# Gate projections of two branches by seven block products, in a two-layer trunk on one core

## The chip, the cores and the metric

The kernel is one program on one core of a Trainium2 chip. Its engines run their own instruction streams in order and meet at semaphores: PE (TensorE, the matmuls; its weight loads are shown as PEld), DVE (VectorE), ACT (ScalarE), POOL (GpSimd) and SP (SyncE, which issues all DMAs here). The metric is device time in microseconds (us): the median of three runs of the kernel before is 2673.18 us (2672.58 to 2675.56).

## The reference, cut to what matters

Two layers, each with 1024 tokens and width 1024. Three branches (g = 0, 1, 2) give `y_g` of width 512 each; a sigmoid gate per branch and output column weighs their projections.

```
h = rms_norm(x, norm_w);  p = h @ w_in                      # [1024, 1024] @ [1024, 9180]
... y_a, y_b, y_c from p: sparse attention (g 0), stick-breaking attention (g 1), mLSTM (g 2)
proj  = einsum('bsgc,gcd->bsgd', branches, w_branch)
gates = sigmoid(merge.reshape(b, s, 3, 1024))               # merge: the last 3 * 1024 columns of p
mixed = sum(gates * proj, axis=2)
x     = x + mixed @ w_out
```

So the gates are three products of 1024 x 1024 by 1024 x 1024 per layer that need nothing but `h`.

## The kernel before, in words

**Arithmetic.** A float32 matrix is cut into a high part of type fp32r and a low part (the rest). A product is three passes, high by high, high by low and low by high (`PASSES`), all summed in one bank of PSUM. With blocks of 128 on the contraction, a tile of 128 columns by 512 tokens takes 24 matmuls of 128x512 (8 blocks, 3 passes), or 12 over half of the contraction. Cutting a tile costs a copy on ACT (the high part; the profile shows it as CAST) and two subtractions of 128x256 on POOL (`pool_tt`; the low part).

**Stages of a layer.** Small projections and index scores (p1); mLSTM and, beside it, a search for thresholds on DVE and ACT (p2); stick-breaking attention (p3); sparse attention (p4); then the branch projections, times the gates, and the output product, which is done in seven block products already (p5). `h`, transposed and cut, stays in SBUF as `hT`: in each of two parts eight blocks of 128 by two halves of 512 tokens (`mov(b, k, th)`).

**The work ahead.** The gates depend on `h` alone, so the 24 matmuls of each gate tile are done while attention runs, as work that PE takes when nothing more urgent is ready. There are 48 such tiles a layer (3 branches, 8 column blocks `d`, 2 token halves `th`), 1152 matmuls. They have two PSUM banks of their own (`psf`) and ten SBUF tiles (`fill`). The gate goes through a sigmoid on ACT and into DRAM (`gate_d`), and is read back in p5.

**The order.** The body is not issued as it runs. It is recorded as a list (`Log`), and a planner (`Plan.run`) then plays the list through with costs for each operation, gives out buffers, and fixes one order per engine. Among what is ready an engine takes the lowest key. For work ahead on PE the key is its place in the list plus `AHEAD_SHIFT`, so it comes behind nearly all else; on the other engines the key is its bare place. `Plan.emit` issues all of it from one line, so nearly every row of the profile names L533; the shape and the type tell the operations apart. In names, `t` is a tile of its own, `s` a large tile that two halves share, `d` a tile in DRAM.

Of the kernel before, what the change touches and what calls it, by code (L numbers as in the profile page):

```python
# [23 lines left out]
DEPTH = 2  # L24
N_HALF = 21
N_SLAB = 35
N_FILL = 10
N_PSF = 2
TK_ACT = (3, 4, 5)
EPS = 1e-6  # L30
# [3 lines left out]
PASSES = ((0, 0), (0, 1), (1, 0))  # L34
# [3 lines left out]
C_MLQ, C_MLK, C_MLV, C_IF, C_MLO, C_MLZ, C_MERGE = 3540, 4052, 4564, 5076, 5084, 5596, 6108  # L38
# [49 lines left out]
MARGIN = {"half": 2, "slab": 2}  # L88
STEP = 100
SPARE = {"ps": 2}  # L90
AHEAD = (2, 1, 0)
AHEAD_SHIFT = 7700
LOOK = {"half": 400, "slab": 400, "ps": 300}
EXTRA = 0.0
# [117 lines left out]
class Plan:  # L212
# [3 lines left out]
    def __init__(self, log, info, caps):  # L216
        self.info, self.caps = info, caps
        prio = log.prio
        ops = []
        n = len(log)  # L220
        self.deps = [set() for _ in range(n)]
        acc, users = {}, {}
        for k, (eng, meth, args, kw) in enumerate(log):
            o = Op()
            o.eng, o.meth, o.args, o.kw = eng, meth, args, kw
            ins, outs = operands(meth, args, kw)
            o.cost = cost(eng, meth, args, kw, ins, outs)
            o.table = table_of(args) if eng == "ACT" else None
            o.port = holds_port(eng, meth, args, kw, ins, outs)
            o.bytes = nbytes(outs[0]) if eng == "SP" else 0  # L230
            o.tiles = []
            ops.append(o)
            for wr, lst in ((False, ins), (True, outs)):
                for a in lst:
                    nm = a.tensor.name
                    if nm not in info:
                        continue
                    if nm not in o.tiles:
                        o.tiles.append(nm)
# [12 lines left out]
        for r, k in enumerate(by):  # L252
            at[k] = r
        self.ops = [ops[k] for k in by]
        self.deps = [{at[k2] for k2 in self.deps[k]} for k in by]
        self.users = {nm: sorted(at[k] for k in u) for nm, u in users.items()}
        self.early = {at[k] for k in log.early}
        self.prio = [prio[k] for k in by]
        self.place = by
        self.n = n  # L260
        for k, d in enumerate(self.deps):
            if d and max(d) > k:
                raise ValueError("the priorities do not follow the data")

    def run(self):
        n, ops, info, caps = self.n, self.ops, self.info, self.caps
# [3 lines left out]
            for k2 in d:  # L270
                succ[k2].append(k)
        pri, early = self.prio, self.early
        key = [pri[k] if k not in early or ops[k].eng == "PE" else self.place[k] for k in range(n)]
        first = {nm: u[0] for nm, u in self.users.items()}
        last = {nm: u[-1] for nm, u in self.users.items()}
        left = {nm: len(u) for nm, u in self.users.items()}
# [2 lines left out]
        for nm in left:  # L279
            c = info[nm][1]  # L280
# [20 lines left out]
        f = 0  # L301
# [312 lines left out]
def body(log, tiles, caps, x_in, w_in, w_uk, w_uv, kvn, conv_w, ib, fb, mln, w_br, w_out, nrm, fnrm,  # L614
         rope_t, out, stop=None, dbg=None):
    V, S, G, PE, SY = (Engine(log, e) for e in ("DVE", "ACT", "POOL", "PE", "SP"))
# [9 lines left out]
    def half(dt=F32, n=520):  # L626
        return tiles.new("half", [128, n], dt)
# [5 lines left out]
    def fill(dt=F32):  # L633
        return tiles.new("fill", [128, 512], dt)
# [151 lines left out]
    for tb in range(8):  # L786
        x = slab()
# [13 lines left out]
    for l in range(DEPTH):  # L801
        wl = w_in[l]

        def cols(c, n, _w=wl):
            return _w[:, c:c + n]

        def mov(b, k, th, _h=hT):
            return _h[b][k][th][:, :512]
# [51 lines left out]
        for i in range(4):  # L860
# [8 lines left out]
            d = ikd[i // 2][:, (i % 2) * 256:(i % 2) * 256 + 256].rearrange("p (t e c) -> p t e c", t=2, e=2)  # L869
# [13 lines left out]
        for tb in range(2, 8):  # L883
            v = iq[tb // 2][:, (tb % 2) * 256:(tb % 2) * 256 + 256].rearrange("p (h c) -> p h c", h=4)
            q = half(F32R)
# [3 lines left out]
            p = pst("tr")  # L889
# [29 lines left out]
        for th in range(2):  # L919
            ss = small([128, 8], name="ssk", bufs=2)  # L920
            for j in range(2):
                w = pb[2 * th + j][:, :424].rearrange("p (t c) -> p t c", t=2)[:, :, 0:128]
                q = half()
# [5 lines left out]
            p = pst("tr")  # L929
# [6 lines left out]
            q = half()  # L936
# [101 lines left out]
            SY.dma_start(f(y_d[g][0][blk][:, t0:t0 + n]), f(hi[:, :n]))  # L1038
            SY.dma_start(f(y_d[g][1][blk][:, t0:t0 + n]), f(lo[:, :n]))

        gate_d = {}
        log.ahead, log.shift = True, AHEAD_SHIFT
        for g in AHEAD:
            for d in range(8):
                W = [[], []]
                for hb in range(2):
                    st, wh, wl_ = fill(), fill(F32R), fill(F32R)
                    SY.dma_start(st[:, :512].rearrange("p (k c) -> p k c", k=4),
                                 cols(C_MERGE + g * 1024 + d * 128, 128)[hb * 512:hb * 512 + 512, :]
                                 .rearrange("(k p) c -> p k c", p=128))  # L1050
                    S.copy(wh[:, :512], st[:, :512])
                    pool_tt(wl_, st, f(wh), ALU.subtract, 512)
                    W[0].append(wh)
                    W[1].append(wl_)
                for th in range(2):
                    p = pst("psf")
                    i = 0
                    for a, b in PASSES:
                        for k in range(8):
                            PE.matmul(p, W[a][k // 4][:, (k % 4) * 128:(k % 4) * 128 + 128], mov(b, k, th),  # L1060
                                      start=(i == 0), stop=(i == 23))
                            i += 1
                    t = fill()
                    S.activation(t[:, :512], p, AF.Sigmoid)
                    gate_d[g, d, th] = dram([128, 512])
                    SY.dma_start(gate_d[g, d, th], t[:, :512])
        log.ahead, log.shift = False, 0

        if stop == "p1":
# [25 lines left out]
        p = pst("tr")  # L1095
# [5 lines left out]
        p = pst("tr")  # L1101
# [8 lines left out]
        p = pst("tr")  # L1110
# [21 lines left out]
        p = pst("tr")  # L1132
# [7 lines left out]
        for h in range(4):  # L1140
            W1 = load_w([(cols(C_MLQ + h * 128, 128), 0), (cols(C_MLK + h * 128, 128), 128)])
            cv = {}
            for j in range(2):
                raw = [half(), half()]
                for th in range(2):
                    p = pst("mm")
# [6 lines left out]
                for th in range(2):  # L1153
                    a = half()
                    blk = 4 * j + h
# [10 lines left out]
            if h % 2 == 0:  # L1166
                W2 = load_w([(cols(C_MLV + h * 128, 256), 0)])
                vq = []
                for q in range(4):
                    p = pst("mm")  # L1170
# [418 lines left out]
            return g, p  # L1589

        def wm(g, ct):
            return (None if g in AHEAD else load_w([(cols(C_MERGE + g * 1024 + ct * 256, 256), 0)]),
                    load_w([(w_br[l, g][:, ct * 256:ct * 256 + 256], 0)], nk=4))

        last = l == DEPTH - 1
# [142 lines left out]
```

## Time and profile before

| | |
|---|---|
| median of 3 runs | 2673.18 us |
| profiled execution | 2675.59 us, its span 2673.8 us |
| PE busy | 2641.5 us, 99% |
| DVE, ACT, POOL busy | 1749.8, 1466.0, 1100.4 us (65, 55, 41%) |
| DMA | 243.16 MB on SP's queue, 29.5% of 16 engines |
| granted TensorE clock, mean over the span | 0.999 of full speed |

Busy time of PE runs from the start of a matmul to its modelled end, and the next one starts before that end, so a row's mean for one matmul is longer than the step from one matmul to the next. The step is read from a stretch in which PE does one kind of work without a break. A wait that is shorter than the overlap of two matmuls shows as busy PE.

### The profile page before, as it was taken

The numbers are of one execution on the slowest core, as the hardware profiler recorded it, in microseconds if no ns is written. First come the engines' busy times: TensorE is split into PE (matmuls) and PEld (weight loads), VectorE is DVE, ScalarE is ACT, GpSimd is POOL, SyncE is SP. The second block draws the span as 40 slices with busy tenths as digits, with TensorE's granted clock in tenths as the row PEclk, the third lists the DMA queues.
The fourth block names the chain that finished last, engine by engine and source line by source line (L and its number), as shares of the span: only waits on it lengthen the run. The fifth ranks groups of instructions, "written<-read, shape, count | busy, mean of one in ns | idle before, by whom it ended". The sixth has DMA issues, their size and how long they took to land.

```text
span 2673.8 us, 41885 instructions
## 1 busy us (share of the span) xinstructions
PE 2641.5 (99%) x14676; PEld 2233.9 (84%) x14676; DVE 1749.8 (65%) x4059; ACT 1466.0 (55%) x2971; POOL 1100.4 (41%) x1445
## 2 busy tenths in 40 slices
PE   8999999999999999999999999999999999999998
PEld 7888888888888888888898888888888878888886
DVE  5829789667596753426866397996666776723278
ACT  4737873545476866512445469634556577764123
POOL 4343344332342534444814253432342444433536
PEclk9999999999999999999999999999999999999999
DMA  4322232212132315564204132231111322256531
GB/s 126 90 51 68 76 79 68 64 52 69 35 94 64 89 55 185 192 222 150 69 25 121 32 103 52 68 93 51 55 57 34 98 76 79 65 173 234 176 118 71
DMA packets 252550, 245.83 MB, mean 92 GB/s; under 512 B 23514, under 2 KB 198580, under 8 KB 252340
## 3 DMA queue, kind: packets, MB, share of 16 engines
q1 hardware_dynamic: 252340, 243.16, 29.5%
q8 instruction: 116, 1.90, 0.3%
q14 instruction: 94, 0.77, 0.1%
HBM read 180.84 MB, written 62.26 MB: 91 GB/s over the span
## 4 chain that ended last, share of the span: by engine, by line
PE 90%; DVE 4%; ACT 3%; issue 2%; POOL 0%; DMA 0%; POOLq 0%; ACTq 0%; DVEq 0%
PE t L533 90%; DVE t L533 4%; ACT t L533 3%; POOL t L533 0%; ACT L533 0%; DMA t<-in_w_in_dram 0%; ACT s L533 0%; DMA t<-in_x_dram 0%; DVE s L533 0%; POOLq L1734 0%; ACTq L533 0%; DVEq L533 0%; POOLq L533 0%
## 5 line engine op out<-in xcount | busy, mean ns | idle before, releaser
L533 PE MATMUL t<-t,t 128*128 128x512 f32 (+5 forms) x13802 | 2497.4, 342 | 22.4 <-DVE t L533 10.0
L533 PEld LDWEIGHTS t<-t,t 128*128 128x128 f32 (+2 forms) x13674 | 2080.1, 183 | 384.2 <-DVE t L533 23.3
L533 POOL TENSOR_TENSOR t<-t,t 128x256 fp32r<-128x256 f32 (+5 forms) x956 | 767.9, 833 | 1006.5 <-ACT t L533 409.0
L533 DVE TENSOR_TENSOR t<-t,t 128x512 f32<-128x512 f32 (+12 forms) x1454 | 725.9, 528 | 586.1 <-ACT t L533 470.7
L533 ACT CAST t<-t 128x512 fp32r<-128x512 f32 (+6 forms) x991 | 504.0, 549 | 456.8 <-PE t L533 222.3
L533 ACT ACTIVATE t<-t 128x512 f32<-128x512 f32 (+5 forms) x697 | 343.3, 579 | 266.6 <-PE t L533 210.9
L533 ACT ACTIVATE t<-t,t 128x1024 bf16<-128x1024 f32 (+10 forms) x352 | 307.9, 887 | 61.0 <-DVE t L533 34.2
L533 ACT COPY t<-t 64x256 f32<-64x256 f32 (+4 forms) x300 | 113.0, 379 | 250.9 <-PE t L533 248.6
L533 DVE TENSOR_TENSOR_SCAN t<-t 128x256 f32<-128x256 f32 (+10 forms) x144 | 205.0, 1436 | 8.8 <-ACT t L533 8.6
L533 POOL TENSOR_SCALAR t<-t 64x512 fp32r<-64x512 f32 x128 | 83.2, 650 | 247.2 <-ACT t L533 169.4
L533 DVE SCALAR_TENSOR_TENSOR t<-t,t,t 128x512 f32<-128x512 f32 (+8 forms) x217 | 160.0, 766 | 18.0 <-ACT t L533 11.2
L533 PE MATMUL t<-s,t 128*128 128x512 f32 (+1 forms) x474 | 149.1, 385 | 0.0
L533 DVE TENSOR_SCALAR_CACHE_REDUCE t<-t,t 128x512 bf16<-128x512 f32 (+5 forms) x198 | 145.8, 763 | 1.1
L533 ACT ACT_TABLE_LOAD x105 | 134.7, 1283 | 14.0 <-PE t L533 6.6
L533 POOL TENSOR_SCALAR t<-t,t 128x128 f32<-128x128 f32 (+7 forms) x128 | 94.8, 749 | 110.4 <-DVE t L533 107.3
L533 DVE TENSOR_TENSOR s<-s,t 128x512 f32<-128x512 f32 (+1 forms) x98 | 69.3, 709 | 106.7 <-PE t L533 97.8
L533 DVE CUSTOM_DVE_ANT_0 t<-t,t 128x512 f32<-128x512 f32 (+3 forms) x160 | 92.1, 591 | 18.0 <-PE t L533 9.4
L533 PEld LDWEIGHTS t<-s,t 128*128 128x128 f32 x474 | 87.4, 188 | 19.0
L533 POOL TENSOR_TENSOR t<-s,s 128x256 fp32r<-128x256 f32 x50 | 52.5, 1075 | 44.8 <-issue 30.6
L533 DVE TENSOR_SCALAR t<-t,t 128x512 f32<-128x512 f32 (+12 forms) x94 | 52.8, 573 | 19.2 <-ACT t L533 11.0
L533 DVE TENSOR_SCALAR t<-t 128x1 f32<-128x1 f32 (+5 forms) x324 | 58.8, 190 | 5.9 <-ACT t L533 3.7
L533 DVE TENSOR_TENSOR t<-t 128x1 f32<-128x1 f32 (+6 forms) x224 | 59.0, 272 | 3.7 <-POOL t L533 1.0
(53 smaller groups left out, 811.5 us busy)
## 6 DMA issues: line engine op xcount, KB each, us to landing
t<-in_w_in_dram SPq DMA_DIRECT2D x192, 256.0 KB, 3.7
d<-t SPq DMA_DIRECT2D x134, 256.0 KB, 2.0
t<-d SPq DMA_DIRECT2D x133, 256.0 KB, 5.2
s<-d SPq DMA_DIRECT2D x103, 256.0 KB, 5.3
t<-in_w_in_dram SPq DMA_DIRECT2D x44, 512.0 KB, 5.2
d<-t SPq DMA_DIRECT2D x130, 128.0 KB, 1.8
t<-in_w_branch_dram SPq DMA_DIRECT2D x24, 512.0 KB, 6.0
t<-in_x_dram SPq DMA_DIRECT2D x16, 512.0 KB, 5.6
```

The costliest lines, as they stand in the source:

```text
L533: fn(*args, **kw)
```

## The change

Branch 2 (`PLAIN`) keeps its 24 matmuls a tile. For branches 1 and 0 (`AHEAD`) column blocks `d` and `d + 4` are taken as a pair, so that the product is one of 2 x 2 blocks: two halves of the columns, two of the contraction, two of the tokens. It is done in seven products of 12 matmuls in place of eight.

- Four sums of blocks of `h` (S0 to S3 here, each of four 128x512 blocks, cut into high and low) are made at the start of a layer, at four places 1200 list entries apart (`SUM_SHIFT`), and kept in DRAM (`s_d`): 64 subtractions and additions of 128x256 on POOL, 16 copies on ACT, 24 operations of 128x512 on DVE and 32 stores a layer.
- For each of the eight pairs (2 branches, 4 `d`) the sums of weights are made by POOL, cut, and partly kept in DRAM (`t1_d`, `t2_d`). Products that belong to several outputs (`p_d`, `u_d`, `v_d`) go to DRAM and come back: copied into the PSUM bank by ACT ahead of the matmuls (`S.copy(X, t)`), or added by DVE behind them (`back`).
- The products run in four phases over all eight pairs, each with one sum in the same eight `half` tiles (`ts`), which are loaded again for each phase (`sums_of`).
- Work ahead on ACT, DVE, POOL and SP gets a key that is spread over the stretch from 700 to 7800 entries behind the block (`Plan.spread`) in place of its bare place. `N_FILL` rises from 10 to 12.

```diff
-N_FILL = 10
+N_FILL = 12
...
-AHEAD = (2, 1, 0)
+PLAIN = (2,)
+AHEAD = ((1, 0),)
+SUM_SHIFT = 1200
+LATER = 0
+SPREAD = (700, 7800)
...
+    def spread(self, c):
+        a, z = next((a, z) for a, z in self.blocks if a <= c < z)
+        return z + SPREAD[0] + (c - a) / (z - a) * (SPREAD[1] - SPREAD[0])
...
-        key = [pri[k] if k not in early or ops[k].eng == "PE" else self.place[k] for k in range(n)]
+        key = [pri[k] if k not in early or ops[k].eng == "PE" else self.spread(self.place[k]) for k in range(n)]
...
+        for k in range(4):
+            log.shift = SUM_SHIFT * (k + 1)
...
+            t = both(a21, a22, ALU.add)
+            keep(1, k, t)
...
-                W = [[], []]
-                for hb in range(2):
-                    st, wh, wl_ = fill(), fill(F32R), fill(F32R)
...
+                W = [cut_w(raw(g, d, hb)) for hb in range(2)]
...
+        for gs in AHEAD:
+            pairs = [(g, d) for g in gs for d in range(4)]
+            for g, d in pairs:
+                W1 = cut_w(raw(g, d, 0))
+                Z = pst("psf")
+                gprod(Z, W1, blk(0, 0))
+                t = fill()
+                S.copy(t, Z)
+                put(p_d, (g, d), t)
+                W2 = cut_w(raw(g, d, 1))
+                gprod(Z, W2, blk(0, 4), False)
+                close((g, d, 0), Z, fill())
+            ts = [(half(F32R)[:, :512], half(F32R)[:, :512]) for _ in range(4)]
+            Sm = sums_of(0, ts)
+            for g, d in pairs:
+                r11, r12, r22 = raw(g, d, 0), raw(g, d + 4, 0), raw(g, d + 4, 1)
+                add(r12, r12, r11, ALU.subtract)
+                put(t1_d, (g, d), r12)
+                add(r12, r22, r12, ALU.subtract)
+                put(t2_d, (g, d), r12)
+                W6 = cut_w(r12)
+                X = pst("psf")
+                t = fill()
+                SY.dma_start(t, p_d[g, d])
+                S.copy(X, t)
+                gprod(X, W6, Sm, False)
+                S.copy(t, X)
+                put(u_d, (g, d), t)
+            Sm = sums_of(1, ts)
+            for g, d in pairs:
+                W5 = cut_w(bring(t1_d[g, d]))
+                X = pst("psf")
+                gprod(X, W5, Sm)
+                put(v_d, (g, d), back(X, u_d[g, d]))
+            Sm = sums_of(2, ts)
...
+            Sm = sums_of(3, ts)
...
+                S.copy(X, t)
+                gprod(X, W3, Sm, False)
+                close((g, d + 4, 0), X, t)
```

Where the order moves, first on PE, before: a piece of stick-breaking attention in the first layer with work ahead between. Each row is output <- moving operand, weights; `t410` is a `psf` bank, `t43` to `t57` are the high parts of `hT`, `t406` and `t409` low parts of weights, `t1862` holds attention logits.

```order
L533 MATMUL t410_7981<-t57_253,t408_7993 128x512
L533 MATMUL t410_7981<-t43_217,t406_7937 128x512 [waits Pool_49]
L533 MATMUL t410_7981<-t47_228,t406_7937 128x512 [waits Pool_49]
L533 MATMUL t410_7981<-t51_240,t409_8037 128x512 [waits Pool_49]
L533 MATMUL t1862_8075<-t1747_7607,t1751_7670 128x128 [waits DVE_49]
L533 MATMUL t1862_8075<-t1747_7607,t1752_7675 128x128
L533 LDWEIGHTS t2_96
L533 MATMUL t1862_8075<-t3_98,t2_96 128x128
```

The moving operand of the work ahead is always `hT`, which is there from the start of the layer, and what it waits for is cut weights.

On PE now, at the first change from S0 to S1 in the same part of the program. `s536`, `s538` and `t540` are three of the eight tiles of the sum, `t621` is the last bank of phase S0, `t627` and `t633` are the first two of phase S1, `t2099` to `t2139` are attention.

```order
L544 MATMUL t621_8623<-s536_1542,t620_8747 128x512 [waits Pool_49]
L544 MATMUL t621_8623<-s538_2263,t620_8747 128x512
L544 MATMUL t2129_8825<-t2011_8188,t2015_8273 128x256 [waits DVE_49]
L544 MATMUL t2099_8799<-t1_92,t2094_8664 128x128 [waits DVE_49]
L544 MATMUL t2098_8852<-t2100_8839,t1943_7800 128x256 [waits Activation_49]
L544 MATMUL t627_8858<-s536_1542,t625_8671 128x512 [waits DMAHW4_49]
L544 MATMUL t627_8858<-s538_2263,t625_8671 128x512 [waits DMAHW5_49]
L544 MATMUL t627_8858<-t540_3962,t625_8671 128x512 [waits DMAHW6_49]
L544 MATMUL t633_8867<-s536_1542,t631_8781 128x512
L544 MATMUL t2139_8882<-t2011_8188,t2015_8273 128x384 [waits PE_49,Activation_49]
```

Rows that repeat are left out; between the last read of the old `s536` and the first of the new one PE has 18 matmuls in all: three of 128x512, two of 128x256, one small one, eleven of 128x128 and one more of 128x256. The first row of the new phase waits for a DMA.

On SP now, the loads of S1 at that place. The first two columns of a row's operands are target and source; `d` is DRAM, and `t646` and the stores belong to other work.

```order
L544 DMA s536_1542<-d284_1476 128x512 [waits DMAHW6_49,PE_49]
L544 DMA s538_2263<-d285_2176 128x512 [waits DMAHW7_49,PE_49]
L544 DMA d262_8103<-t2067_8712 128x256 [waits DMAHW0_49,Pool_49]
L544 DMA t541_3983<-d286_3852 128x512 [waits DMAHW1_49,PE_49]
L544 DMA t543_6079<-d287_6003 128x512 [waits DMAHW2_49,PE_49]
L544 DMA t646_8784<-d583_8471 128x512 [waits DMAHW3_49,Pool_49]
L544 DMA s536_1542<-d280_1454 128x512 [waits DMAHW4_49,PE_49]
L544 DMA s538_2263<-d281_2146 128x512 [waits DMAHW5_49,PE_49]
L544 DMA t540_3962<-d282_3819 128x512 [waits DMAHW6_49,PE_49]
L544 DMA d623_8823<-t622_8514 128x512 [waits DMAHW7_49,Activation_49]
L544 DMA t542_6072<-d283_5970 128x512 [waits DMAHW0_49,PE_49]
```

Each of the eight loads waits for the last matmul that reads the old tile, and stands in one queue with stores that wait for ACT and POOL. Such a change from one sum to the next comes three times a layer; the sums themselves and their loads are new.

## Rows read from the trace of the kernel before

**Rows 1.** The page's first part: busy us, share, instructions of each engine.

```profile
PE 2641.5 (99%) x14676; PEld 2233.9 (84%) x14676; DVE 1749.8 (65%) x4059; ACT 1466.0 (55%) x2971; POOL 1100.4 (41%) x1445
```

**Rows 2.** The chain that ended last, by engine.

```profile
PE 90%; DVE 4%; ACT 3%; issue 2%; POOL 0%; DMA 0%; POOLq 0%; ACTq 0%; DVEq 0%
```

**Rows 3.** Windows: the output product of layer one; busy us (x instructions), clock, DMA.

```profile
core 0: us, PE busy (x) PEld busy (x) DVE busy (x) ACT busy (x) POOL busy (x), PEclk, DMA share, GB/s
1203.00:1270.00 67.00, 67.00 (x290) 54.19 (x289) 43.10 (x61) 13.99 (x22) 28.00 (x36) 1.00 0.45 150
```

**Rows 4.** Lines by form, PE's costliest: busy us, mean ns, idle before, releasers.

```profile
L533 PE MATMUL t<-t,t 128*128 128x512 f32 x6968 | 1823.0, 402 | 4.3 <-ACT t L533 2.7 <-DVE t L533 1.0 <-POOL t L533 0.3
```

**Rows 5.** Timeline of PE, runs of narrow matmuls: start, us, row, count.

```profile
19.81 2.63 PE L533 MATMUL t<-t,t 128*128 128x256 f32 x21
...
342.47 1.28 PE L533 MATMUL t<-t,t 128*128 128x128 f32 x10
```

**Rows 6.** Waits, of weight loads: us in total, times, longest.

```profile
PEld t L533 <- DVE t L533: 23.3, 58, 3.4
PEld t L533 <- ACT t L533: 22.5, 66, 1.9
...
PEld t L533 <- POOL t L533: 13.2, 35, 1.9
```

**Rows 7.** DMA issues by kind: count, KB each, median us to landing.

```profile
t<-in_w_in_dram SPq DMA_DIRECT2D x192, 256.0 KB, 3.7
d<-t SPq DMA_DIRECT2D x134, 256.0 KB, 2.0
t<-d SPq DMA_DIRECT2D x133, 256.0 KB, 5.2
```

**Rows 8.** DMA queue of SP: packets, MB, share of 16 engines.

```profile
q1 hardware_dynamic: 252340, 243.16, 29.5%
```

**Rows 9.** Lines by form on POOL, ACT and DVE, of the kinds that are added.

```profile
L533 POOL TENSOR_TENSOR t<-t,t 128x256 fp32r<-128x256 f32 x712 | 619.1, 896 | 717.6 <-ACT t L533 390.3 <-PE t L533 196.4 <-DMA d<-t 64.0
...
L533 ACT CAST t<-t 128x512 fp32r<-128x512 f32 x359 | 209.9, 612 | 97.7 <-PE t L533 50.7 <-DVE t L533 26.1 <-DMA d<-t 10.7
L533 DVE TENSOR_TENSOR t<-t,t 128x512 f32<-128x512 f32 x242 | 173.4, 721 | 243.9 <-ACT t L533 170.9 <-PE t L533 69.8 <-DMA t<-in_w_out_dram 2.1
...
L533 ACT ACT_TABLE_LOAD x105 | 134.7, 1283 | 14.0 <-PE t L533 6.6 <-DVE t L533 3.4 <-issue 1.3
...
L533 POOL TENSOR_TENSOR t<-t,t 128x256 f32<-128x256 f32 x56 | 39.0, 719 | 126.1 <-DVE t L533 120.2 <-DMA t<-d 5.9
...
L533 ACT COPY t<-t 128x512 f32<-128x512 f32 x48 | 27.9, 582 | 58.8 <-PE t L533 58.8
```

**Rows 10.** Lines by form: DVE with one operand in PSUM, and with none.

```profile
L533 DVE TENSOR_TENSOR s<-s,t 128x512 f32<-128x512 f32 x91 | 63.6, 700 | 106.2 <-PE t L533 97.3 <-DMA t<-d 4.2 <-POOL s L533 2.2
...
L533 DVE TENSOR_TENSOR s<-s,s 128x512 f32<-128x512 f32 x32 | 24.3, 776 | 0.4
```

**Rows 11.** Windows, the busiest stretch of the DMA engines in layer one.

```profile
1100.00:1150.00 50.00, 48.50 (x248) 40.38 (x247) 23.11 (x53) 23.02 (x40) 25.40 (x34) 1.00 0.91 311
```

More of the change, by code (lines that the diff above doesn't have):

```diff
@@ L257, in __init__ @@
         self.early = {at[k] for k in log.early}
+        self.blocks = [(k, next(z for z in range(k, n + 1) if z not in log.early)) for k in log.early
+                       if k - 1 not in log.early]
         self.prio = [prio[k] for k in by]
@@ L1039, in store_y @@
             SY.dma_start(f(y_d[g][1][blk][:, t0:t0 + n]), f(lo[:, :n]))
-        gate_d = {}
-        log.ahead, log.shift = True, AHEAD_SHIFT
-        for g in AHEAD:
-            for d in range(8):
-                W = [[], []]
-                for hb in range(2):
-                    st, wh, wl_ = fill(), fill(F32R), fill(F32R)
[L1048 to L1054, printed above, removed]
+        s_d = [[[dram([128, 512], F32R) for _ in range(4)] for _ in range(2)] for _ in range(4)]
@@ new lines, in keep, with low, both @@
+        def keep(i, k, src):
+            hi, lo = half(F32R)[:, :512], half(F32R)[:, :512]
+            split(src, hi, lo, 512)
+            for q, x in enumerate((hi, lo)):
+                SY.dma_start(f(s_d[i][q][k]), f(x))
+        for k in range(4):
+            log.shift = SUM_SHIFT * (k + 1)
+            a11, a21 = ([f(mov(q, k, th)) for q in range(2)] for th in range(2))
+            a12, a22 = ([f(mov(q, 4 + k, th)) for q in range(2)] for th in range(2))
+            def low(x, y, op):
+                t = half()[:, :512]
+                pool_tt(t, x[1], y[1], op, 512)
+                return t
+            def both(x, y, op):
+                u = low(x, y, op)
+                t = half()[:, :512]
+                V.tensor_tensor(t, x[0], y[0], op)
+                V.tensor_tensor(t, t, u, ALU.add)
+                return t
+            t = both(a21, a22, ALU.add)
+            keep(1, k, t)
+            V.tensor_tensor(t, t, a11[0], ALU.subtract)
+            pool_tt(t, t, a11[1], ALU.subtract, 512)
+            keep(0, k, t)
+            log.shift += LATER
+            V.tensor_tensor(t, a12[0], t, ALU.subtract)
+            pool_tt(t, t, a12[1], ALU.add, 512)
+            keep(3, k, t)
+            keep(2, k, both(a11, a21, ALU.subtract))
@@ new lines, in body, with raw, add, cut_w @@
+        gate_d, p_d, u_d, v_d, t1_d, t2_d = {}, {}, {}, {}, {}, {}
+        log.ahead, log.shift = True, AHEAD_SHIFT
+        def raw(g, d, hb):
+            t = fill()
+            SY.dma_start(t.rearrange("p (k c) -> p k c", k=4),
+                         cols(C_MERGE + g * 1024 + d * 128, 128)[hb * 512:hb * 512 + 512, :]
+                         .rearrange("(k p) c -> p k c", p=128))
+            return t
+        def add(dst, x, y, op):
+            pool_tt(dst, x, y, op, 512)
+        def cut_w(t):
+            hi, lo = fill(F32R), fill(F32R)
+            S.copy(hi, t)
+            pool_tt(lo, t, f(hi), ALU.subtract, 512)
+            return hi, lo
@@ new lines, in gprod, with sums_of @@
+        def gprod(p, W, B, first=True):
+            i = 0
+            for a, b in PASSES:
+                for k in range(4):
+                    PE.matmul(p, W[a][:, k * 128:k * 128 + 128], B(b, k), start=first and i == 0, stop=i == 11,
+                              skip_group_check=True)
+                    i += 1
+        def sums_of(i, ts):
+            for k in range(4):
+                for q in range(2):
+                    SY.dma_start(f(ts[k][q]), f(s_d[i][q][k]))
+            return lambda b, k: ts[k][b]
@@ new lines, in put, with close, back, bring @@
+        def put(dct, key, t):
+            dct[key] = dram([128, 512])
+            SY.dma_start(dct[key], t)
+        def close(key, src, t):
+            S.activation(t, src, AF.Sigmoid)
+            put(gate_d, key, t)
+        def back(p, kept):
+            t = fill()
+            SY.dma_start(t, kept)
+            V.tensor_tensor(t, p, t, ALU.add)
+            return t
+        def bring(kept):
+            t = fill()
+            SY.dma_start(t, kept)
+            return t
+        def blk(th, o):
+            return lambda b, k: mov(b, o + k, th)
@@ L1055, in body @@
+        for g in PLAIN:
+            for d in range(8):
+                W = [cut_w(raw(g, d, hb)) for hb in range(2)]
                 for th in range(2):
@@ L1059, in body @@
                         for k in range(8):
-                            PE.matmul(p, W[a][k // 4][:, (k % 4) * 128:(k % 4) * 128 + 128], mov(b, k, th),
+                            PE.matmul(p, W[k // 4][a][:, (k % 4) * 128:(k % 4) * 128 + 128], mov(b, k, th),
                                       start=(i == 0), stop=(i == 23))
                             i += 1
-                    t = fill()
-                    S.activation(t[:, :512], p, AF.Sigmoid)
-                    gate_d[g, d, th] = dram([128, 512])
@@ L1066, in body @@
-                    SY.dma_start(gate_d[g, d, th], t[:, :512])
+                    close((g, d, th), p, fill())
+        for gs in AHEAD:
[4 more added lines that the diff above has]
+                gprod(Z, W1, blk(0, 0))
+                t = fill()
+                S.copy(t, Z)
[13 more added lines that the diff above has]
+                X = pst("psf")
+                t = fill()
+                SY.dma_start(t, p_d[g, d])
[10 more added lines that the diff above has]
+            Sm = sums_of(2, ts)
+            for g, d in pairs:
+                r12, r22 = raw(g, d + 4, 0), raw(g, d + 4, 1)
+                add(r12, r22, r12, ALU.subtract)
+                W7 = cut_w(r12)
+                r21, t2 = raw(g, d, 1), bring(t2_d[g, d])
+                add(r21, r21, t2, ALU.subtract)
+                W4 = cut_w(r21)
+                Y = pst("psf")
+                gprod(Y, W7, Sm)
+                t = back(Y, v_d[g, d])
+                close((g, d + 4, 1), t, t)
+                gprod(Y, W4, blk(1, 4), False)
+                t = back(Y, u_d[g, d])
+                close((g, d, 1), t, t)
+            Sm = sums_of(3, ts)
+            for g, d in pairs:
+                W3 = cut_w(raw(g, d + 4, 1))
+                X = pst("psf")
+                t = fill()
+                SY.dma_start(t, v_d[g, d])
+                S.copy(X, t)
+                gprod(X, W3, Sm, False)
+                close((g, d + 4, 0), X, t)
@@ L1591, in wm @@
         def wm(g, ct):
-            return (None if g in AHEAD else load_w([(cols(C_MERGE + g * 1024 + ct * 256, 256), 0)]),
+            return (None if g in PLAIN or any(g in x for x in AHEAD) else load_w([(cols(C_MERGE + g * 1024 + ct * 256, 256), 0)]),
                     load_w([(w_br[l, g][:, ct * 256:ct * 256 + 256], 0)], nk=4))
```

## The prediction

> **What bounds the kernel now.** I read the busy times first. PE is busy for 2641.5 of 2673.8 us, and no other engine for more than 65% [rows 1]. A busy share can hide waits, so the chain of waits comes next: 90% of the chain that ended last is PE itself, with 4% on DVE and 3% on ACT [rows 2]. Time is thus taken away by taking work from PE, as long as what PE has left can still fill its stream. The price of one matmul of the gates is then needed. The row of its kind says 402 ns [rows 4], but that is from start to modelled end, and matmuls overlap; the step is read from a stretch with nothing but such matmuls and no break: 290 in 67.00 us, 231 ns each, at a granted clock of 1.00 of full speed, the 2.4 GHz level [rows 3]. The waits of weight loads show how PE is late where it is late: 23.3 us on DVE, 22.5 on ACT and 13.2 on POOL, 59.0 us in 159 waits, 0.37 us each [rows 6]. DMA engines have room on the average, 29.5% [rows 8].
>
> **PE's work.** Per layer the gates took 48 tiles by 24 matmuls, 1152. Now 16 tiles of branch 2 take 384 and eight pairs take 7 products by 12 matmuls, 672; together 1056. In two layers 192 fewer, and 192 by 231 ns [rows 3] is **-44.4 us**. The new sums cost PE nothing, since DVE and POOL make them. The count is in the program's order, so this is certain; what is not is how much comes back as waits. If the gates' matmuls were only in gaps of PE, taking some away would give nothing; against that stands that PE has but 32.3 us (2673.8 less 2641.5) without a matmul in flight [rows 1], and the gates as a whole take 2304 by 231 ns, 532 us. They are not in gaps left over, they take time of their own.
>
> **The changes of sums.** New is that PE's moving operand can be late. At a change from one sum to the next a tile is loaded again only after its last reader on PE is through, and the first reader of the new content then waits for that DMA. In the place shown in the order of SP and PE, 18 matmuls stand between: three of 128x512 at 231 ns, three of 128x256 at 125 ns (2.63 us for 21) and twelve narrower ones at 128 ns (1.28 us for 10) [rows 3, 5], 2.6 us of work. A 256 KB load from a DRAM tile lands 5.2 us after its issue [rows 7], so PE is 2.6 us late. Counted in the same way, the shortest of the other five changes have 4.0 and 4.1 us of work between (1.2 and 1.1 us late), and three have 5.8 us or more. In sum **+5 us**. Lower end 0 (the stretch of attention runs late anyway, and covers it), upper end below, as a rival. In this stretch every row behind the waiting matmul waits too, attention's transposes with it, and so do ACT and DVE behind those.
>
> **More waits of the work ahead.** In PE's order 113 matmuls of the work ahead waited for something; now 292 do, and all of PE's waiting matmuls rise from 2853 to 3065. Where the data are in time, such a wait is no gap. By the low end each of the 212 costs what all 2853 cost on the average in the shown waits: 59.0 us over 2853, 21 ns [rows 6], 4 us in all; by the high end each is a visible one of 0.37 us, 78 us. The new ones are not like the average: 48 are the sums' own (counted above), and some 60 wait for a copy into the bank, or for an addition out of it, which was finished just before. I take half of these as visible, 30 by 0.37, **+11 us**, nearer the low end, since two banks take turns.
>
> **Work beside PE.** Counted from the order, in both layers: POOL gets 352 operations of 128x256 (128 for the sums of h, 128 for the sums of weights, 96 more low parts), at 719 to 896 ns [rows 9] 253 to 315 us, which brings it to 51 or 53% of the span. ACT gets 144 copies of 128x512 at 582 to 612 ns, some 86 us, and loses 5 of 105 table loads at 1.28 us [rows 9]: to 58%. DVE gets 96 at 721 ns, 69 us: to 68%. None becomes the bound. If PE's waits grow with the busy time of the engine waited for, DVE's 23.3 us grow by 4%, ACT's 22.5 by 5% and POOL's 13.2 by up to 29% [rows 6]: 0.9, 1.2 and 3.8, **+6 us**. The lower end is 0 or below: work ahead on ACT, POOL and SP has a later key than before and stands less in the way of attention's own copies; no row tells how much, and 6 us (what ACT's five table loads save) is my bound for that gain. The cover for all this work is the gates' matmuls themselves; where none is ready, the added 0.7 us pieces show in full.
>
> **DMA.** 400 issues are added, nearly all of 256 KB, 105 MB on 243. At the same cost per byte the queue goes from 29.5 to 42% [rows 8]. In the busiest stretch, at the end of layer one's attention, the engines are at 0.91 with 311 GB/s, and PE still does 248 matmuls in that 50 us with 48.5 us busy [rows 11]; this says that loads of the branch projections come ahead of their use. The reloads of p, u, v and t1, t2 have 5 us or more of PE's work between issue and use in nearly all places. I cost them at nothing, with the prefetch as cover; without it, each would be a wait of up to 5.2 us.
>
> **The sum**: -44.4 + 5 + 11 + 6 = -22.4 us. The profiled execution took 2675.6 us (its span 2673.8, and 1.8 around it), so 2653.2 us; the median of the runs lies 2.4 us lower than that execution, which gives 2650.8. I say **2652 us**, a little more, since waits of separate causes can add to one another in an engine's queue.
>
> The end on the good side comes from the low ends: -44.4 + 0 + 4 + 0, less up to 6 us, is 2627 to 2633 on the median's scale.
>
> **A rule against the change.** DVE's operations with one operand in PSUM take 700 ns for 128x512, those with both in SBUF 776 [rows 10]: 76 ns more, and POOL is busy 41% of the time. The Trainium skill ("SBUF — State Buffer", section "Who interferes with whom") says that an operation of DVE with two inputs in SBUF shares its second read port with GpSimd, and that whichever comes first holds up the other for a whole instruction. By that rule, the trace agrees in the sign of those 76 ns, and some 300 us more of POOL's reads would hold up attention's multiplications on DVE. It gives the slow rival below.
>
> **The rivals.**
> - *All of it arrives.* The added waits lie under matmuls that are ready, and the later keys help. For it: in the dense stretch PE needs nothing of the others for 67 us [rows 3]. Against it: 179 more waits in the work ahead itself. Time 2627 to 2638.
> - *The reloads eat it.* A phase can't go on before all eight tiles of a sum are there. Eight loads are 2.1 MB; at 311 GB/s and 0.91 [rows 11], 342 GB/s with all engines, they take 6.1 us, and with 5.2 us for the landing [rows 7] about 11 us pass without work ahead; SP's queue puts stores that wait for ACT and POOL between them. If attention leaves PE idle for two thirds of this, six changes cost some 44 us instead of 5: about 2673 with the other terms near their low ends. For it: the order has stretches of 30 rows and more behind a change with no work ahead in them. Against it: attention has matmuls there, and two of three rows belong to it.
> - *POOL holds up DVE* (the slow side). 253 to 315 us more of POOL [rows 9], with DVE busy 65% of the time [rows 1], meet DVE for about 180 us; if half of a meeting is waited out, DVE's chains in attention get some 90 us longer. Up to 22 us of this reaching PE leaves the kernel as it was; beyond a quarter it is slower. With half of it reaching PE, 45 us, the time is 2652 - 6 + 45 = 2691. For it: 4% of the chain is DVE, and PE's longest sum of waits is on DVE [rows 2, 6]. Against it: much of DVE's work reads PSUM, and PE has work ahead to take in the meantime.
> - That the change does not do what it says is left out: the order has exactly 192 matmuls fewer.
>
> **How the numbers follow.** About 0.2% either way (5.3 us) can't be told from no change. The forecast, 2641 to 2668, has 0.55; all of it arriving 0.13; the reloads eating it (2668 to 2679) 0.17; the slow side 0.15. Faster: 0.55 and 0.13, with 0.68; same 0.17; slower 0.15. The likeliest case's own range is 2641 to 2668. The range of 2632 to 2690 leaves out the better half of the good rival and about half of the slow one.
>
> **What would show it.** In the profile after: 192 matmuls fewer in PE's count, and 231 ns again in the output product. At the six changes of sums, matmuls of 128x512 that wait for a DMA from a DRAM tile, 1 to 3 us each in three of them and nothing in the others; over 5 us in most would be the second rival. Waits of weight loads on ACT, DVE and POOL of 70 to 85 us in all. DVE's two-operand rows at 721 and 776 ns within some 5%; 10% more, with PE's waits on DVE doubled, would be the third. The forecast is wrong if PE's time without a matmul in flight grows by over 35 us, or not at all.

## The result, and the profile after

The changed kernel takes **2713.22 us** (median of 3; 2710.89 to 2715.89) where the kernel before takes 2673.18: a ratio of 1.0142 (95% interval 1.0128 to 1.0157), 40 us slower. The forecast was 2652 us, with a range up to 2690. Wrong in sign.

The page of the changed kernel: busy us of each engine, the chain by engine, SP's queue (packets, MB, share).

```profile
PE 2629.5 (97%) x14484; PEld 2201.2 (81%) x14484; DVE 1827.0 (67%) x4155; ACT 1543.8 (57%) x3110; POOL 1377.8 (51%) x1797
...
q1 hardware_dynamic: 340660, 348.04, 41.0%
...
PE 77%; ACT 7%; DMA 6%; DVE 4%; POOL 3%; issue 3%; SPq 1%; POOLq 0%; ACTq 0%; DVEq 0%
```

PE has 192 matmuls fewer, as counted. Its busy time fell by only 12 us where 192 steps are 44; the other 32 are longer steps, by the half clock below and by waits too short to show as idle time, and no row separates the two. The time with no matmul in flight went from 32.3 us [rows 1] to 2714.1 - 2629.5 = 84.6, which is 52 more; over 35 more was the prediction's own sign of being wrong. PE's part of the chain fell from 90% [rows 2] to 77%, and ACT, POOL and DMA came in. The shares of ACT, DVE, POOL and DMA are within one point of the forecast (58, 68, 51 to 53 and 42%).

The output product of layer one in the changed kernel, as in [rows 3], and its weight loads' waits, as in [rows 6], with three waits of other engines:

```profile
core 0: us, PE busy (x) PEld busy (x) DVE busy (x) ACT busy (x) POOL busy (x), PEclk, DMA share, GB/s
1221.00:1289.00 68.00, 68.00 (x295) 55.04 (x295) 39.57 (x54) 9.87 (x15) 38.17 (x48) 1.00 0.44 144
```

```profile
POOL t L544 <- DMA d<-t: 119.1, 27, 17.9
...
ACT t L544 <- POOL t L544: 70.1, 50, 5.5
DVE t L544 <- POOL t L544: 66.8, 39, 6.7
PEld t L544 <- ACT t L544: 61.9, 125, 2.2
PEld t L544 <- DVE t L544: 53.2, 87, 3.3
...
PEld t L544 <- POOL t L544: 25.5, 63, 1.7
```

A matmul's step is still 68.00 / 295 = 231 ns, so the work itself is no dearer. The visible waits of weight loads rose from 59.0 us in 159 [rows 6] to 140.6 us in 275: 116 more, and longer ones, 0.51 us in place of 0.37. In the kernel before, ACT and DVE waited less for POOL, so the three engines now hold one another up more:

```profile
DVE t L533 <- POOL t L533: 26.6, 24, 2.8
...
ACT t L533 <- POOL t L533: 6.5, 12, 1.2
```

**Where it happens.** In the last head pair of stick-breaking attention, layer one, DVE is nearly full, and attention alone cannot feed PE. The same 250 rows of attention in the two kernels (windows; the columns are those above):

```profile
720.00:784.00 64.00, 63.51 (x377) 52.17 (x376) 60.38 (x99) 50.16 (x121) 31.09 (x27) 1.00 0.25 79
```

```profile
762.00:833.00 71.00, 59.94 (x331) 47.73 (x330) 61.20 (x102) 50.71 (x120) 33.88 (x31) 0.93 0.52 166
```

Before (the first fence), DVE is busy for 60.38 of 64 us, and 377 - 250 = 127 matmuls of work ahead fill PE beside it. In the changed kernel only some 81 come in between, the stretch takes 7 us more, and PE has 11 us with nothing in flight. What it waits for there, on a small scale (timelines of POOL, ACT and PE in the changed kernel, in one stretch of 10 us; the last bracket is the idle time before a row and its releaser):

```profile
769.67 4.56 POOL L544 TENSOR_TENSOR t<-t,t 128x256 f32<-128x256 f32 x2 [2.98 <-DMA d<-t]
...
774.09 0.62 ACT L544 CAST t<-t 128x512 fp32r<-128x512 f32 x1 [2.20 <-DMA d<-t]
...
775.76 0.90 PE L544 MATMUL t<-s,t 128*128 128x512 f32 x2 [2.04 <-ACT t L544]
```

POOL adds one weight block to another, in two halves, after a wait of 3 us for a store. ACT waits 2.2 us before its next cut; the profile puts this down to a store, but POOL's addition ends at the same moment (769.67 + 4.56 = 774.23 us), so it may be what ACT waited for. PE's next matmul of work ahead has waited 2 us for ACT, with attention's rows behind it.

**The clock.** The granted clock, 0.999 of full speed over the whole span before, falls in three stretches of the changed kernel:

```profile
746.00:814.00 68.00, 60.29 (x329) 49.39 (x327) 55.36 (x96) 47.15 (x110) 30.40 (x26) 0.92 0.52 163
...
1086.00:1153.00 67.00, 64.05 (x355) 52.11 (x355) 47.06 (x146) 55.32 (x110) 36.81 (x52) 0.97 0.78 262
...
2103.00:2171.00 68.00, 59.73 (x335) 47.36 (x334) 64.13 (x105) 51.11 (x124) 26.64 (x25) 0.92 0.48 155
```

Part of each of these stretches ran at 1.2 GHz in place of 2.4. The first has two such falls, with windows at 1.00 between them:

```profile
776.00:782.00 6.00, 6.00 (x33) 5.40 (x33) 3.68 (x7) 5.23 (x14) 2.92 (x5) 0.72 0.33 118
...
806.00:812.00 6.00, 4.65 (x16) 3.41 (x16) 3.62 (x10) 4.33 (x9) 3.58 (x5) 0.57 0.57 209
```

What is missing to a full clock, 0.08 of 68, 0.03 of 67 and 0.08 of 68 us, is about 13 us, and that is the most that the clock can have cost here, since PE was not busy all the time. In the first and last row PE had nothing in flight for 8 us of the 68. No run sets this price apart from that of the waits themselves. The clock of other runs below goes with their time: 0.999 over the whole span in the plain tiles, 0.996 to 0.997 in the bare form, 0.995 with weights cut again, 0.988 to 0.990 without reloads. So some of each loss below can be the clock's: up to 7 of the bare form's 27 us, and up to 11 of the 44 us of cutting again.

### The profile page after: what moved, and what is told of

Read it like the earlier page. It is cut to its first block, busy times and chain, and to the rows that moved or that the text cites. A ratio compares the mean times of both kernels' runs of the same rounds, so it can differ in the third digit from the quotient of the medians.

```text
span 2714.1 us, 43046 instructions
## 1 busy us (share of the span) xinstructions
PE 2629.5 (97%) x14484; PEld 2201.2 (81%) x14484; DVE 1827.0 (67%) x4155; ACT 1543.8 (57%) x3110; POOL 1377.8 (51%) x1797
## 4 chain that ended last, share of the span: by engine, by line
PE 77%; ACT 7%; DMA 6%; DVE 4%; POOL 3%; issue 3%; SPq 1%; POOLq 0%; ACTq 0%; DVEq 0%
PE t L544 77%; ACT t L544 6%; DVE t L544 4%; POOL t L544 3%; DMA t<-in_w_in_dram 2%; DMA d<-t 2%; DMA t<-d 1%; ACT L544 1%; SPq L544 1%; DMA t<-in_w_branch_dram 0%; ACT s L544 0%; DMA s<-d 0%; DVE s L544 0%; DMA t<-in_x_dram 0%; ACTq L544 0%
## 5 line engine op out<-in xcount | busy, mean ns | idle before, releaser
L544 PEld LDWEIGHTS t<-t,t 128*128 128x128 f32 (+1 forms) x13054 | 1978.3, 183 | 430.6 <-ACT t L544 55.4
L544 POOL TENSOR_TENSOR t<-t,t 128x256 fp32r<-128x256 f32 (+5 forms) x1273 | 1017.3, 830 | 931.0 <-ACT t L544 298.2
L544 DVE TENSOR_TENSOR t<-t,t 128x512 f32<-128x512 f32 (+15 forms) x1525 | 790.6, 549 | 539.3 <-ACT t L544 375.0
L544 ACT CAST t<-t 128x512 fp32r<-128x512 f32 (+4 forms) x1071 | 555.2, 555 | 510.2 <-PE t L544 233.5
L544 ACT ACTIVATE t<-t 128x512 f32<-128x512 f32 (+4 forms) x692 | 344.0, 566 | 234.1 <-PE t L544 149.8
L544 ACT ACTIVATE t<-t,t 128x1024 bf16<-128x1024 f32 (+12 forms) x343 | 303.9, 896 | 41.4 <-DVE t L544 19.8
L544 PE MATMUL t<-s,t 128*128 128x512 f32 (+2 forms) x868 | 288.7, 396 | 7.8 <-ACT t L544 3.3
L544 DVE SCALAR_TENSOR_TENSOR t<-t,t,t 128x512 f32<-128x512 f32 (+9 forms) x216 | 168.3, 806 | 15.9 <-ACT t L544 11.0
L544 DVE TENSOR_SCALAR_CACHE_REDUCE t<-t,t 128x384 bf16<-128x384 f32 (+5 forms) x193 | 141.6, 764 | 1.0
L544 POOL TENSOR_SCALAR t<-t,t 128x384 f32<-128x384 f32 (+7 forms) x128 | 95.6, 758 | 48.4 <-DVE t L544 45.5
```

What stands on the lines that cost most here:

```text
L544: fn(*args, **kw)
```

## The experiments

Every kernel here gets its own order from the planner, so a small edit moves many rows. Three edits that leave the work alone (the spread keys by themselves, 14 fill tiles in the kernel before, another tile for a sum) moved the time by 0.1% or less. That is how little a new order can do by itself; it is no bound, so a step of a few us between two kernels is weak evidence. All ratios are to the kernel before, run on the same chip, with 95% intervals; 1% is 27 us.

**Spread keys alone.** `PLAIN = (2, 1, 0)`, `AHEAD = ()`, no sums.

> All three branches as 24 matmuls a tile, no sums; only the later, spread keys of the work ahead and 12 fill tiles are left of the change. PE's count is that of the kernel before. If the later keys starve PE: slower than before by 10 us or more, with waits of weight loads on ACT and POOL near the 62 and 26 us of the changed kernel. If they are harmless (my reading): 2665 to 2680.

2674.21 us, ratio 0.9994 (0.9984 to 1.0003). The keys are harmless.

**Sums alone.** As that, with the sums made.

> As the run before, and the four sums of h are made and kept in DRAM in both layers, but nothing reads them. If the sums' work on POOL, DVE and ACT (64, 24 and 16 operations a layer) holds up the stages that it falls in: 10 us or more over the run with the spread keys alone. If it is hidden: within 4 us of that run.

2689.94 us, 1.0050 (1.0035 to 1.0065): 0.56% or 15 us over the run with the keys alone. The making of the sums is not hidden in this kernel. ACT's waits on POOL are 39.2 us there, after 10.9.

**Without reloads.**

```diff
-            return lambda b, k: ts[k][b]
+            return blk(i % 2, 4 * (i // 2))
```

> The changed kernel, but the products read blocks of h where they should read the sums (the outputs are not the reference's); the sums are made and kept, and never loaded again, so that no matmul waits for a reload. Theory A (the reloads and the stretches without work ahead behind them cost most of the 84 us of new waits, with the fall of the clock that they bring): 2665 to 2680, half-clock stretches gone. Theory B (the weights' side: POOL waits for stores before it may write a tile again, ACT waits for POOL, PE for ACT): 2700 or more.

2735.17 us, 1.0219 (1.0202 to 1.0237): slower than the change itself, and the clock is lower yet (0.988 to 0.990). Theory A falls. The edit does more than take reloads away: the sums' eight of the 21 `half` tiles are free for the rest of the kernel.

**Plain weights.**

```diff
-                W6 = cut_w(r12)
+                W6 = cut_w(raw(g, d + 4, 0))
...
-                W5 = cut_w(bring(t1_d[g, d]))
+                W5 = cut_w(raw(g, d + 4, 0))
```

> The changed kernel, but the products take plain weights where they should take sums of weights (the outputs are not the reference's): no additions of weights on POOL, no t1 and t2 in DRAM, fewer loads; the sums of h and their reloads stay. Theory B: 2650 to 2675, POOL's waits for stores from 119 us down to some 65 us, ACT's on POOL from 70 to under 20 us. Theory A: 2700 or more.

2728.88 us, 1.0196 (1.0181 to 1.0211). ACT's waits on POOL stayed at 71.0 us. Theory B falls too. What both runs keep is the shape of the products: 12 matmuls to a group, and partial products that go out of a bank and come back. Theory C takes the second; the next run checks the dense price.

**Fewer matmuls, plain tiles.** Branches 1 and 0 in tiles of 24, one tile of four in 12:

```diff
+                        gprod(Z, W[0], blk(th, 0))
+                        if e == d or th == 0:
+                            gprod(Z, W[1], blk(th, 4), False)
```

> No sums, no exchange, no phases: the 24-matmul tiles of before, but in branches 1 and 0 one of four tiles (second column half, second token half) leaves out half of its contraction, so that there are exactly the 192 matmuls fewer of the change (the outputs are not the reference's). If PE's work is worth its dense price (the -44 us of the forecast): 2628 to 2640. Rival (the gates are filler, and with less of it PE stands in its gaps): 2660 or more.

2635.14 us, 0.9852 (0.9837 to 0.9866), 40 us less. The page of this run:

```profile
PE 2598.3 (99%) x14484; PEld 2198.9 (83%) x14484; DVE 1735.7 (66%) x4059; ACT 1467.6 (56%) x2969; POOL 1105.5 (42%) x1445
```

The span is 2633.9 us, so 35.6 us have nothing in flight, 3 more than before. The 192 matmuls are worth 90% of their dense price in this form.

**No exchange.** No p, u, v.

```diff
-                S.copy(X, t)
-                gprod(X, W6, Sm, False)
-                S.copy(t, X)
-                put(u_d, (g, d), t)
+                gprod(X, W6, Sm)
+                close((g, d + 4, 1), X, fill())
```

> The changed kernel with sums, reloads, sums of weights and the same 84 matmuls a pair, but partial products are not exchanged: no p, u, v in DRAM, no copy of them into a bank, no addition behind it; each bank is closed by a sigmoid, and the product over S1 is thrown away (the outputs are not the reference's). Theory C (work ahead that hands its banks to ACT and DVE every 12 matmuls makes PE, ACT and DVE wait for one another, which costs most of the 84 us): 2640 to 2665. Rival (sums, reloads and POOL's load): 2695 or more.

2675.94 us, 1.0005 (0.9996 to 1.0015): 1.37% or 37 us below the change. Short of what theory C asked for: the exchange is half of the loss, not most of it.

**Exchange alone.** The tiles of before in two halves of 12, the first by way of DRAM.

> All 24 matmuls of each tile, as before, no sums of any kind; but in branches 1 and 0 each tile is done in two halves of 12, and the first half goes by ACT into DRAM and comes back by ACT into the bank, 32 copies out and 32 in a layer (the change has 16 and 16, and 24 additions on DVE). Theory C: 2700 to 2740, from before's 2676 with the same PE work. Rival (the exchange is hidden): within 8 us of before.

2693.99 us, 1.0074 (1.0057 to 1.0091): +20 us with PE's work unchanged; the same part, seen from the other side, and again under the 26 us at least that were expected.

**Three banks.** `N_PSF = 3`.

> The changed kernel with three banks for the work ahead in place of two, and five for the rest (four are needed at most). Theory C, if it is the turn of the banks: 2685 or less. If it is not the banks but the queues of ACT and DVE: 2705 to 2725. If the rest misses its sixth bank more: slower still.

2746.18 us, 1.0268 (1.0253 to 1.0284). That is the third case: by this reading the rest of the kernel misses its sixth bank more than the work ahead gains by a third. The run does not separate the two.

**No exchange, no reload.**

> As the run without exchange (2676), and the products read blocks of h in place of the sums, which are made and kept, but never loaded (the outputs are not the reference's). Left beside the 192 matmuls fewer are the making of the sums (14 us by itself) and the sums of weights. If reloads are what is left of the cost: 2650 to 2655. If they are not: 2668 or more.

2665.27 us, 0.9955 (0.9940 to 0.9970): 0.50% or 13 us below the run without exchange. Between the two expectations. As above, eight `half` tiles come free with the reloads, so the 13 us are not the reloads' alone.

**No exchange, plain weights.**

> As the run without exchange (2676), and plain weights in place of sums of weights (the outputs are not the reference's); sums of h and their reloads stay. If POOL's additions, the stores of t1 and t2 and the second and third loads of the same weights are what is left: 2650 to 2660. If it is the reloads: 2668 or more.

2669.14 us, 0.9977 (0.9967 to 0.9987): 0.28% or 8 us. Here neither case came: the sums of weights cost little.

**Bare form.** No exchange, no sums, no reloads.

> As the run without exchange, and without sums of h, reloads and sums of weights: only the seven products of 12 matmuls in four phases are left, with four sigmoids a pair (the outputs are not the reference's). 2632 to 2645, near the 2635 of the plain tiles with as many matmuls; if groups of 12 and the order in phases cost by themselves: 2650 or more.

2664.00 us, 0.9953 (0.9938 to 0.9968): 1.01% or 27 us slower than plain tiles with exactly as many matmuls. The form costs by itself. Beside the run without exchange and reloads (0.9955), which still makes the sums of h and of weights, it is no faster: here those sums cost nothing that the runs can tell. Its page:

```profile
PE 2612.6 (98%) x14484; PEld 2205.1 (83%) x14484; DVE 1750.4 (66%) x4059; ACT 1484.8 (56%) x3010; POOL 1184.7 (45%) x1541
```

POOL has 96 operations more than with plain tiles: 48 more cuts of a weight tile. Theory F, which runs below test, says that the loss comes of this: each cut tile now feeds 12 matmuls where it fed 24.

**Old keys in the change.** `self.place[k]` again.

> The changed kernel with the old keys: work ahead on ACT, DVE, POOL and SP at its bare place, so ahead of nearly all else. If the spread keys make work ahead late (and so the stretch in which DVE is the bound short of it): 2690 or less. If they keep it out of attention's way, as meant: 2725 or more.

2732.21 us, 1.0201 (1.0184 to 1.0218): 16 us worse. With this much work beside PE the spread keys help.

**Plain tiles, cut again.** Weights loaded and cut for each token half.

```diff
-                    W = [cut_w(raw(g, e, hb)) for hb in range(2)]
...
+                        gprod(Z, cut_w(raw(g, e, 0)), blk(th, 0))
```

> The plain tiles with 192 matmuls fewer (2635 us), but weights of branches 1 and 0 are loaded and cut anew for each token half, so that each cut tile feeds 12 matmuls, 7 cuts a pair as in the seven-product form (the outputs are not the reference's). Theory F: 2655 to 2670, like the bare form. Rival (the order in phases, not the cutting): 2633 to 2642.

2679.12 us, 1.0017 (1.0008 to 1.0027): 1.65% or 44 us over the plain tiles, for nothing but loading and cutting weights twice as often per matmul. The weight loads' waits of the plain tiles, then of these:

```profile
PEld t L544 <- ACT t L544: 24.2, 70, 1.9
...
PEld t L544 <- DVE t L544: 21.7, 44, 3.4
PEld t L544 <- POOL t L544: 15.0, 36, 1.3
```

```profile
PEld t L544 <- DVE t L544: 38.2, 73, 3.3
PEld t L544 <- ACT t L544: 38.2, 99, 1.9
...
PEld t L544 <- POOL t L544: 28.7, 55, 3.5
```

60.9 us become 105.1, and ACT's waits on POOL go from 14.7 to 57.7 us. The order in phases is not needed for the loss; with as many cuts it is 0.64% better than this. No run has the loads without the cuts.

**Bare form, more fill tiles.** `N_FILL = 16`, `N_SLAB = 33`.

> The bare seven-product form (2664 us) with 16 fill tiles in place of 12 and 33 large tiles in place of 35 (the outputs are not the reference's). Theory F, if the stock of ready work is short: 2640 to 2655. If it is the cutting itself, or if the missing large tiles cost more: 2660 or more.

2648.35 us, 0.9898 (0.9884 to 0.9913): 15 us of the 27 come back, so the stock of ready work is about half of the form's cost. Plain tiles were not run with 16 fill tiles; the kernel before gains nothing from 14 (below).

**Before, fewer fill tiles.** `N_FILL = 6`.

> The kernel before with 6 fill tiles in place of 10, all else alike. Theory F, stock: 2690 to 2710, since half as many matmuls are ready at a time. If the stock does not matter (the cutting does, or neither): within 6 us of before.

2683.90 us, 1.0033 (1.0020 to 1.0046): the sign expected, less than the size; 9 us.

**The change, more fill tiles.**

> The changed kernel with 16 fill tiles in place of 12 and 33 large tiles in place of 35. Theory F, stock: 2685 to 2700, from 2713. If the stock is not what it lacks: 2708 to 2730.

2726.86 us, 1.0193 (1.0178 to 1.0208): 14 us worse. It may be that two large tiles fewer cost the whole change more than four fill tiles give; the two were not changed one at a time.

**Before, 14 fill tiles.** `N_SLAB = 34`.

> The kernel before with 14 fill tiles in place of 10 and 34 large tiles in place of 35. If more ready work helps the kernel before as it helped the bare form: 2660 to 2670. If ten tiles are enough for cut tiles that feed 24 matmuls: within 5 us of before.

2678.75 us, 1.0008 (0.9999 to 1.0017). Ten seem to be enough for tiles that feed 24 matmuls; a gain can be hidden by the large tile that is gone.

**Another tile for the second sum.**

```diff
-                add(r12, r12, r11, ALU.subtract)
-                put(t1_d, (g, d), r12)
-                add(r12, r22, r12, ALU.subtract)
+                add(r11, r12, r11, ALU.subtract)
+                put(t1_d, (g, d), r11)
+                add(r12, r22, r11, ALU.subtract)
```

> The changed kernel, but the first sum of weights goes into another tile than the second, so that POOL writes the second without waiting for the store of the first. If these waits count: 2700 or less, and POOL's waits for stores fall from 119 us to under 90. If they are hidden: 2708 to 2718.

2713.15 us, 1.0137 (1.0124 to 1.0151). POOL's waits for stores were still 118.8 us, so the edit did not take them away, and the run does not say what they are worth. Their total does not go with the time, though; the plain tiles, the fastest kernel here (2635 us), have more of them:

```profile
POOL t L544 <- DMA d<-t: 131.4, 16, 33.7
```

No version that computes the reference beat the kernel before.

## Why the prediction was wrong

- **PE's work, -44.4 us: right.** Plain tiles with the same 192 matmuls fewer gained 40 us.
- **More waits of the work ahead, +11 us: this step failed.** It counted PE's waiting rows and priced them as late ends of a copy. It said nothing of how fast work ahead can be made ready. The bare form alone, with no partial product out of a bank or back, costs 27 us, and loading and cutting weights for every 12 matmuls in plain tiles 44: twelve matmuls are 2.8 us of PE's work, for which ACT and POOL have to cut a tile (0.6 us and twice 0.9 [rows 9]) in the middle of attention's own copies. Half as many matmuls per cut tile are ready when DVE holds attention up; that this is the reason is supported by the fill tiles (16 gave the bare form 15 us back, 6 cost the kernel before 9), not read from rows. Then the exchange costs 37 us more on top of everything else, and 20 by itself. Removed from the whole change, it leaves 2676 us; the term of 11 had it in with the rest.
- **Work beside PE, +6 us: mis-sized.** The busy shares came out as forecast, but waits did not grow with them. The sums of h alone cost 15 us in the old tiles: with POOL's share at 45% in place of 41, ACT's waits on POOL went from 10.9 to 39.2 us. The price is not a fixed one, though: in the seven-product form without exchange and reloads, the sums of h and of weights together cost nothing that can be told (0.9955 with them, 0.9953 without).
- **The changes of sums, +5 us: the wait was about right.** PE's waits for reloads in the changed kernel:

```profile
PE t L544 <- DMA s<-d: 2.1, 4, 0.8
...
PE t L544 <- DMA t<-d: 0.9, 2, 0.8
```

That is 3.0 us, at three of the six changes (1.1, 0.8 and 1.2 us, at 789, 916 and 2125 us), close to what the prediction said would show. What reloads cost beyond these waits is not settled: taking them away without the exchange gave 13 us back, of which 6.0 are such waits of PE, but it also frees eight `half` tiles; in the whole change it made the kernel slower.
- **DMA at nothing:** its share was right (41.0%), and the loads of the branch projections were no later than before (ACT's waits for them 88.4 us, 90.2 before). POOL's waits for stores rose from 64.0 us to 119.1, but no run shows that this costs time: the plain tiles have 131.4.
- **The rivals.** The slow side was forecast by the wrong mechanism: POOL holding up DVE. DVE's rows in the changed kernel, beside [rows 9] and [rows 10], and POOL's additions:

```profile
L544 DVE TENSOR_TENSOR t<-t,t 128x512 f32<-128x512 f32 x323 | 239.0, 747 | 238.2 <-ACT t L544 109.3 <-PE t L544 77.0 <-POOL t L544 45.5
L544 POOL TENSOR_TENSOR t<-t,t 128x256 f32<-128x256 f32 x236 | 192.9, 840 | 139.6 <-DVE t L544 69.4 <-DMA t<-in_w_in_dram 33.7 <-DMA d<-t 11.4
...
L544 DVE TENSOR_TENSOR s<-s,s 128x512 f32<-128x512 f32 x37 | 28.3, 768 | 2.3 <-POOL t L544 0.6 <-POOL s L544 0.6
```

721 to 747 ns and 776 to 768: within the 5% that was to refute it. The other half of that rival's sign did come: PE's waits on DVE more than doubled, 23.3 to 53.2 us, though no DVE row here is over 4% longer. POOL's additions went from 719 to 840 ns in the mean, but that row now holds 236 in place of 56, most of them new, and POOL's largest row, the low parts, went from 896 [rows 9] to 872. The Trainium skill ("SBUF — State Buffer", section "Who interferes with whom") says that issue order decides which of the two is held up. By the means above neither side is clearly held up here, and no run sets the order of such a pair. The rival of the reloads named the right symptom, stretches of attention with no work ahead in them, and the wrong reason: without any reload the kernel is slower, and PE has 87.3 us with nothing in flight.
- **The sum of the parts**, by ratios to before (the 0.52 in the middle comes with the reloads): -1.48% for the matmuls, +1.01 for the form, +0.52 for sums, reloads and sums of weights, +1.37 for the exchange: +1.42. Each part is the step from one kernel of the study to the next (plain tiles, bare form, no exchange, the change), so they close by themselves; taken in another order the parts would have other sizes, as the exchange's 20 and 37 us show.

What stays open: with the exchange in place, taking away the reloads (+0.77%) or the sums of weights (+0.54%) made it slower, with a lower clock and as much time without a matmul in flight (87.3 and 86.5 us). Work ahead that is no longer held up by loads could come in earlier and meet attention in a worse place; that is an argument, not shown.

## What to carry to other kernels

Work that fills an engine's gaps is worth its dense price only while it is ready. Before cutting it, ask how many of its instructions one prepared tile feeds, how many prepared tiles there are room for, and whether its results leave the engine without waiting for a queue that the main work uses too; fewer matmuls with twice the preparation per matmul can cost more than they save. Busy shares of helper engines do not price this; a run with the reduced work and none of the machinery, and one with the machinery and none of the reduction, do.

## What was not expected of the hardware

The granted clock fell to 1.2 GHz in three stretches in the middle of the changed kernel, twice in the first of them, though PE was still busy there for 60 to 64 of 67 or 68 us, and its longest single time with nothing in flight was 2.0, 0.9 and 2.3 us; in the kernel before no stretch of its middle shows less than 1.00. One POOL addition of 128x256 in the busy stretch took 3.42 us by the timeline, against 0.72 us in the mean before [rows 9]; whether it was held up by DVE was not tried.
